# One queued vector task, not two, behind the turn that follows a mixing step of the attention stage

## The chip, the cores and the metric

The kernel runs on one core of one Trainium2 chip. The metric is the device time of one execution in microseconds (us): the median of several executions. TensorE (PE, with PEld for its weight loads) multiplies matrices, VectorE (DVE) and ScalarE (ACT) work on tiles element by element, GpSimd (POOL) and SyncE (SP) mostly issue transfers. Each engine works off its own queue in order, and the engines wait for each other through semaphores.

## The reference

One encoder layer on 512 tokens of width 2048, all in float32. One input projection gives queries, keys, values and gates of two groups of 16 heads. Group A attends along dilated windows, group B in a two-dimensional neighbourhood; each result is multiplied by a SiLU gate, both go through one output projection, and a residual layer norm follows.

```python
h = jnp.einsum('bsd,de->bse', x, w_in[layer])
qa, ka, va, ga, qb, kb, vb, gb = jnp.split(h, splits, axis=-1)
ya = _dilated_attention(heads(qa, N_HEADS_A), heads(ka, N_HEADS_A), heads(va, N_HEADS_A), t5_bias)
yb = _neighbourhood_attention(heads(qb, N_HEADS_B), heads(kb, N_HEADS_B), heads(vb, N_HEADS_B), na_rpb[layer])
ya = merge(ya) * jax.nn.silu(ga.astype(jnp.float32))
yb = merge(yb) * jax.nn.silu(gb.astype(jnp.float32))
y = jnp.concatenate([ya, yb], axis=-1).astype(x.dtype)
out = jnp.einsum('bse,ed->bsd', y, w_out[layer])
x = _layer_norm(DEEPNORM_ALPHA * x + out, ln_gain[layer], ln_bias[layer])
```

## The kernel before

Float32 operands are kept as two parts, a high one and a low one (`split`: the high part is a rounded copy made by ACT, the low part the remainder made by DVE), and a product is three matmuls: high times high, high times low, low times high.

The program has three stages. The first computes the projections (lines 279 to 407 of the matmuls). The second, from 595.5 us on, is the attention stage, which the change touches. The third finishes the output projection and the layer norm.

The attention stage is one loop over 136 steps, `n`. A step handles a quarter of a head: 128 queries. Four steps are a head, eight are a pair of heads, `i = n // 8`; pairs of group A (all 512 keys a query block) and of group B (192 or 256 keys) alternate. Step n holds, in the order of the code:

- the scores of quarter n: two matmuls (lines 677 and 678) into one PSUM bank `sc`, then on DVE one instruction that adds the bias, writes `s` and gives the row minimum `mn` (line 634), and on ACT the exponential (line 638);
- in a mixing step (n % 4 == 2) the weighted values of the head that ended: eight matmuls into a bank `pv` (line 719), a copy of half of it by ACT to `tmp` (line 864), and the sum of both halves by DVE to `y` (line 865);
- the turn of quarter n - 2: the probabilities are transposed on PE into a bank `pt` (line 697), ACT copies them to `th` (line 702), and DVE makes the remainder `tl` (line 703);
- some matmuls of a filler stream (lines 572 and 778): first six gate projections, then the first half of the output projection. They take weights that are loaded ahead and split by ACT (`wh`, line 549) and DVE (`wl`, line 553).

`sc` and `pv` take turns in the same two PSUM banks. So scores need the bank that the bank user before the last one has left free: either line 634 has read that step's scores, or line 865 has read the values.

Small DVE tasks that belong to no step stand in a list `held`, ordered by rank. Rank 1 is the low part of a weight (line 553) and the second half of a gate's SiLU (line 578). Rank 2 is the division of `y` by the softmax denominators (line 751) and the low part of the gated `y` (line 759, which writes the tile `yk`). Rank 4 is the product of `y` with its gate (line 742). `behind_min(k)` takes up to k tasks from the front and issues them at that place of the DVE queue. There are two such places in a group of four steps: a mixing step takes two, between its softmax and its line 865; the step behind it (n % 4 == 3) takes one or two, right behind the low part of its turn. How many the second place takes is the line that changes (872). One more rule sets the latest place of a weight's low part: `prepare`, called before the first matmul of each weight, issues what is due and not done yet.

The engines of this stage are scheduled by hand (`manual_schedule`): instructions stand in each engine's queue as the code issues them.

Of the kernel before, what the change touches and what calls it, by code (L numbers as in the profile page):

```python
# [71 lines left out]
def hybrid_layer(tc, xT, xn, w_in, w_early, w_mid, w_gate, w_out, t5x, brow, rpb, cmask, eye, gain, lbias, out):  # L72
    nc = tc.nc
    from contextlib import ExitStack
    with ExitStack() as ctx:
# [452 lines left out]
        held = []  # L528

        def later(k, fn, dve=False):  # L530


            tasks.setdefault(step[0] + k, []).append((fn, dve))

        def prepare():

            while lows_due:
                low = lows_due.pop(0)
                low()
                held[:] = [h for h in held if h[1] is not low]  # L540
            while stream and len(raws) < 4:
                raws.append(raw_ring.next("wraw"))
                nc.sync.dma_start(raws[-1], stream.pop(0))
            if not raws:
                return
            raw = raws.pop(0)
            h, l = halves.next("wh", F32R), halves.next("wl", F32R)
            ready.append((h, l))
            later(1, lambda: nc.scalar.activation(h, raw, AF.Copy))

            def low():
                if not done:
                    nc.vector.tensor_tensor(l, raw, f(h), ALU.subtract)
                    done.append(True)

            done = []
            lows_due.append(low)
            later(1 if step[0] % 4 else 2, low, 1)
# [31 lines left out]
        def load_kq(i):  # L590

            g, j = ORDER[i]
            t0 = 4 * (i % 2)
            kt = slot(f"t{t0}", F32R, "k").rearrange("p (a n) -> p a n", a=2)
            qt = slot(f"t{t0 + 1}", F32R, "q").rearrange("p (a n) -> p a n", a=2)
            ql = lows[i % 2]

            nc.sync.dma_start(f(kt.rearrange("p a n -> p (a n)")), k_d[g][j].rearrange("c s a q -> (c s) (a q)"))
            for a in range(2):
                nc.sync.dma_start(f(qt[:, a]), _view(q_d[g], (256 * j + 64 * a) * S, [[S, 64], [0, 2], [1, S]]))  # L600
            nc.sync.dma_start(f(ql[0:128:2]), q_d[g][j][1].rearrange("(a c) q -> c a q", a=2))
            loaded[i] = qt, ql, kt

        def load_v(i):


            g, j = ORDER[i]
            vv = slot(f"t{4 * (i % 2) + 2}", F32R, "vv").rearrange("p (b e) -> p b e", b=4)
            if g == 0:
                nc.sync.dma_start(f(vv.rearrange("p b e -> p (b e)")), v_d[g][j].rearrange("p b e -> p (b e)"))  # L610
            else:
                at = j * 128 * 1024
                for p0, c0, n, col, blk in ((0, 0, 4, 8, 0), (64, 0, 3, 0, 1), (64, 3, 1, 0, 0)):
                    nc.sync.dma_start(f(vv[p0:p0 + 64, c0:c0 + n].rearrange("p b e -> p (b e)")),
                                      _view(v_d[g], at + 1024 * col + 256 * blk,
                                            [[16 * 1024, 8], [1024, 8], [1, 256 * n]]))
            vs[i] = vv.rearrange("p b (h e) -> p b h e", h=2)

        def load_sg(i):
            sgs[i] = sg_ring.next("sg")  # L620
            nc.sync.dma_start(sgs[i], sg_d[i])
# [35 lines left out]
        def load_bias(h):  # L657
            g, _, _, hg = head(h)
            bias = two[h % 2]
            n = BW if g else 560  # L660
            nc.sync.dma_start(bias[:, :n], bias_d[g][hg])
            biases[h] = bias

        def scores(n):

            h, b = divmod(n, 4)
            g, i, a, _ = head(h)
            qt, ql, kt = loaded[i]
            cols = slice(128 * b, 128 * b + 128)
            sc = bank(pss, "sc")  # L670
            o, ko = sc, kt[:, a]
            if g:
                rows = "p (r w) -> p r w"
                c0, w = COLS[b]
                o = sc[:, :8 * w].rearrange(rows, r=8)
                ko = ko.rearrange(rows, r=8)[:, :, c0:c0 + w]
            nc.tensor.matmul(o, qt[:, a, cols], ko, start=True, stop=False)  # L677
            nc.tensor.matmul(o, ql[:, a, cols], ko, start=False, stop=True)  # L678
            if g == 0:
                p, exponent = softmax(sc, biases[h][:, 48 - 16 * b:560 - 16 * b], 512, 0, i, 4 * a + b)  # L680
                probs[n] = p, 4
                return exponent
            at = BIAS[(0, 1, 1, 2)[b]][0]
            outer = {0: (64, outers[h % 2][0]), 3: (0, outers[h % 2][1])}
            p, exponent = softmax(sc, biases[h][:, at:at + 8 * w].rearrange(rows, r=8), 8 * w, 1, i, 4 * a + b,
                                  *outer.get(b, ()))
            probs[n] = p, 2
            return exponent
# [36 lines left out]
        def share(i):  # L725

            turn8 = bank(pst, "pt")[0:8, 0:128]
            nc.tensor.transpose(turn8, dens[i], ident)
            rc = rc_ring.next("rc")

            def send():
                nc.scalar.activation(row, turn8, AF.Copy)
                nc.gpsimd.dma_start(rc_d[i], row)
                for a in range(2):
                    nc.gpsimd.dma_start(rc[64 * a:64 * a + 64], _view(rc_d, 1024 * i + 512 * a, [[0, 64], [1, 512]]))
                rcs[i] = rc

            later(0, send)
# [74 lines left out]
        def fill(n):  # L813
            for _ in range(n):
                next(filler, None)
# [4 lines left out]
        def behind_min(n):  # L820

            for _ in range(min(n, len(held))):
                held.pop(0)[1]()

        def close():

            for fn, dve in tasks.pop(step[0], ()):
                if dve and 0 <= step[0] < 134:
                    hold(dve, fn)
                else:  # L830
                    fn()
            step[0] += 1
# [5 lines left out]
        with tc.manual_schedule(engines=engines):  # L838
            prepare()
            for _ in range(3):  # L840
                close()
            while step[0] < 0:
                fill(7)
                close()
            for n in range(136):
                b, i = n % 4, n // 8
                mixing = n % 4 == 2 and 6 <= n <= 130
                amount = ((3, 5, 3, 5) if n < 76 else (5, 6, 4, 6))[b]
                if b == 0 and n < 124:
                    load_bias(n // 4 + 1)  # L850
                if n % 8 == 0 and n < 120:
                    load_kq(i + 1)
                if n % 8 == 4 and n < 128:
                    if n < 120:
                        load_v(i + 1)
                    load_sg(i)
                exponent = scores(n) if n < 128 else None
                if mixing:
                    if exponent:
                        exponent()  # L860
                    behind_min(2)
                    fill(2)
                    mine, theirs, y, t = values(n // 4 - 1)
                    nc.scalar.activation(t, theirs, AF.Copy)
                    nc.vector.tensor_tensor(y, mine, t, ALU.add)
                    fill(amount - 2)
                else:
                    fill(2)
                if 2 <= n < 130:
                    turn(n - 2)  # L870
                if b == 3 or n >= 134:
                    behind_min(99 if n >= 134 else 2 if len(held) > 3 or held and held[0][0] == 1 else 1)
                if not mixing:
                    if exponent:
                        exponent()
                    fill(amount - 2)
                if n >= 8 and n % 8 == 0:
                    later(0, lambda i=i: nc.vector.reciprocal(dens[i - 1], dens[i - 1]))
                if n >= 8 and n % 8 == 1:
                    share(i - 1)  # L880
                if n >= 8 and n % 8 == 4:
                    later(0, lambda i=i: gate(i - 1), 4)
                if n % 8 == 1 and 2 <= i < 2 * PAIRS:
                    gated(i - 2)
                if n % 8 == 7 and i >= 2 * PAIRS - 1:
                    gated(i - 1)
                close()
            for n in (0, 400):
                fill(n)
                while tasks or held:  # L890
                    behind_min(99)
                    close()
# [238 lines left out]
```

## Time and profile before

| | |
|---|---|
| median of 3 executions | 976.0 us (975.39 to 976.22) |
| the profiled execution's own time | 975.37 us |
| its span, first to last instruction | 973.6 us |
| attention loop, scores of step 0 to scores of step 127 | 595.51 to 862.90 us |
| mean granted TensorE clock | 0.998 |
| ACT, POOL busy, share of the span | 501.3 us (51%), 181.2 us (19%) |

A line of the profile's timeline is: start, duration, engine, source line, operation, the tile written and those read, and in brackets the idle time of the engine just before with what ended it. The duration of a matmul is modelled and overlaps with the next one, so that the distance of two starts tells more than the durations. The windows view gives for a stretch of time its length and what each engine was busy in it, with the number of instructions.

### The profile page before, as it was taken

The numbers are of one execution on the slowest core, as the hardware profiler recorded it, in microseconds if no ns is written. First come the engines' busy times: TensorE is split into PE (matmuls) and PEld (weight loads), VectorE is DVE, ScalarE is ACT, GpSimd is POOL, SyncE is SP. The second block draws the span as 40 slices with busy tenths as digits, with TensorE's granted clock in tenths as the row PEclk, the third lists the DMA queues.
The fourth block names the chain that finished last, engine by engine and source line by source line (L and its number), as shares of the span: only waits on it lengthen the run. The fifth ranks groups of instructions, "written<-read, shape, count | busy, mean of one in ns | idle before, by whom it ended". The sixth has DMA issues, their size and how long they took to land.

```text
span 973.6 us, 14211 instructions
## 1 busy us (share of the span) xinstructions
PE 964.5 (99%) x4861; PEld 805.3 (83%) x4861; DVE 767.2 (79%) x1169; ACT 501.3 (51%) x870; POOL 181.2 (19%) x321
## 2 busy tenths in 40 slices
PE   9999999999999999999999999999999999999997
PEld 7878888888888889998888888878888788888886
DVE  7897778779689678788679885788887777777877
ACT  7454444444444344454444544777776776763300
POOL 1006646735646000000000000111111010010020
PEclk9999999999999999999999999999999999999999
DMA  9716797698496086272196178767787668678213
GB/s 341 272 67 136 240 314 209 181 302 231 104 362 197 29 258 162 72 272 87 52 301 179 52 228 269 263 214 256 221 276 217 208 205 241 192 228 296 73 58 116
DMA packets 121255, 194.18 MB, mean 199 GB/s; under 512 B 49551, under 2 KB 70415, under 8 KB 121184
## 3 DMA queue, kind: packets, MB, share of 16 engines
q1 hardware_dynamic: 108672, 170.21, 54.8%
q0 software_dynamic: 11936, 22.42, 8.3%
q8 instruction: 38, 0.62, 0.3%
q10 hardware_dynamic: 576, 0.66, 0.2%
q14 instruction: 33, 0.27, 0.1%
HBM read 148.69 MB, written 44.50 MB: 198 GB/s over the span
## 4 chain that ended last, share of the span: by engine, by line
PE 94%; ACT 2%; DVE 2%; issue 1%; DMA 1%; SPq 0%; DVEq 0%; ACTq 0%
PE acc L405 16%; PE acc L407 16%; PE acc L406 16%; PE acc L778 14%; PE acc L572 6%; PE pv L719 4%; PE pt L697 4%; PE acc L397 2%; PE acc L396 2%; PE acc L395 2%; PE sc L678 2%; PE sc L677 2%; PE pt L260 1%; PE acc L279 1%; PE sc L778 1%; PE acc L280 1%
## 5 line engine op out<-in xcount | busy, mean ns | idle before, releaser
L377 ACT ACTIVATE wh<-braw 128x1024 fp32r<-128x1024 f32 (+1 forms) x196 | 202.1, 1031 | 278.9 <-PE acc L406 205.5
L382 DVE TENSOR_TENSOR wl<-braw,wh 128x1024 fp32r<-128x1024 f32 (+1 forms) x196 | 232.8, 1190 | 59.7 <-ACT wh L377 59.4
L405 PE MATMUL acc<-wh,xk 128*128 128x512 f32 x384 | 151.5, 394 | 0.0
L407 PE MATMUL acc<-wl,xk 128*128 128x512 f32 x384 | 149.9, 390 | 0.0
L406 PE MATMUL acc<-wh,xk 128*128 128x512 f32 x384 | 149.7, 390 | 0.0
L373 DVE TENSOR_TENSOR braw<-braw 128x1024 f32<-128x1024 f32 (+1 forms) x112 | 132.3, 1182 | 0.0
L778 PE MATMUL acc<-wh,yk 128*128 128x512 f32 x320 | 113.5, 407 | 0.0
L405 PE MATMUL acc<-wh,op 128*128 128x512 f32 x288 | 113.3, 393 | 0.0
L407 PE MATMUL acc<-wl,op 128*128 128x512 f32 x288 | 112.4, 390 | 0.0
L406 PE MATMUL acc<-wh,op 128*128 128x512 f32 x288 | 112.2, 390 | 0.0
L703 DVE TENSOR_TENSOR tl<-pt,th 128x256 fp32r<-128x256 f32 (+1 forms) x128 | 71.1, 556 | 29.8 <-ACT th L702 27.9
L407 PEld LDWEIGHTS acc<-wl,xk 128*128 128x128 f32 x384 | 72.1, 188 | 15.3
L405 PEld LDWEIGHTS acc<-wh,xk 128*128 128x128 f32 x384 | 72.2, 188 | 15.2 <-ACT bias L151 0.9
L406 PEld LDWEIGHTS acc<-wh,xk 128*128 128x128 f32 x384 | 72.2, 188 | 14.4
L638 ACT ACTIVATE p<-s,mn 128x512 f32<-128x512 f32 (+1 forms) x96 | 62.5, 651 | 32.9 <-DVE mn L634 32.2
L634 DVE CUSTOM_DVE_ANT_0 s<-sc,biases 128x512 f32<-128x512 f32 (+2 forms) x128 | 67.6, 528 | 11.3 <-PE sc L678 10.9
L702 ACT ACTIVATE th<-pt 128x256 fp32r<-128x256 f32 (+1 forms) x128 | 62.2, 486 | 22.6 <-PE pt L697 21.0
L778 PEld LDWEIGHTS acc<-wh,yk 128*128 128x128 f32 x320 | 58.1, 189 | 8.2 <-ACT wh L88 0.2
L161 POOL DMA_DIRECT2D bias<-rows_d x128 | 61.4, 487 | 15.8 <-DMA rows_d<-bias 5.4
L407 PEld LDWEIGHTS acc<-wl,op 128*128 128x128 f32 x288 | 54.1, 188 | 11.4
L406 PEld LDWEIGHTS acc<-wh,op 128*128 128x128 f32 x288 | 54.2, 188 | 10.9
L405 PEld LDWEIGHTS acc<-wh,op 128*128 128x128 f32 x288 | 54.1, 188 | 10.9
(188 smaller groups left out, 1777.7 us busy)
## 6 DMA issues: line engine op xcount, KB each, us to landing
braw<-in_w_in SPq DMA_DIRECT2D x96, 512.0 KB
wraw<-in_w_out SPq DMA_DIRECT2D x32, 512.0 KB
k_d<-kst SPq DMA_DIRECT2D x64, 128.0 KB
q_d<-kst SPq DMA_DIRECT2D x64, 128.0 KB
v_d<-vst SPq DMA_DIRECT2D x32, 256.0 KB
q<-q_d SPq DMA_DIRECT2D x32, 256.0 KB
k<-k_d SPq DMA_DIRECT2D x16, 512.0 KB
braw<-in_w_mid SPq DMA_DIRECT2D x16, 384.0 KB
```

Source lines behind the costliest of these rows:

```text
L161: nc.gpsimd.dma_start(bt[16 * r:16 * r + 16], _view(rows_d, h * 16 * ROW + 463 - 64 * r, [[ROW - 1, 16], [1, 560]]))
L373: nc.vector.tensor_tensor(raws[q][u], raws[q][u], raws[other][u], ALU.add)
L377: nc.scalar.activation(h, raws[q][u], AF.Copy)
L382: nc.vector.tensor_tensor(l, raws[q][u], f(h), ALU.subtract)
L405: nc.tensor.matmul(accs[t], ah[:, q], h[:, c], start=first and k == 0, stop=False, skip_group_check=skip)
L406: nc.tensor.matmul(accs[t], al[:, q], h[:, c], start=False, stop=False, skip_group_check=skip)
L407: nc.tensor.matmul(accs[t], ah[:, q], l[:, c], start=False, stop=k == 7, skip_group_check=skip)
L634: nc.vector.tensor_tensor_reduce(*flat, bias, 1.0, 3e38, ALU.add, ALU.min, mn)
L638: nc.scalar.activation(p[:, to:to + n].rearrange("p (b r c) -> p b r c", r=8, c=c), s[:, :n].rearrange(order, r=8, c=c), AF.Exp, bias=mn, ...
L702: nc.scalar.activation(th, pt[:, :nch], AF.Copy)
L703: nc.vector.tensor_tensor(tl, pt[:, :nch], f(th), ALU.subtract)
L778: nc.tensor.matmul(acc[:, part], yk[k][:, s, c], w[:, wk], start=first and kk == 0 and n == 0, stop=last and kk == 1 and n == 2)
```

## The change

One condition of the attention loop: how many tasks the step behind a mixing step takes.

```diff
@@ -869,7 +869,7 @@
                 if 2 <= n < 130:
                     turn(n - 2)
                 if b == 3 or n >= 134:
-                    behind_min(99 if n >= 134 else 2 if len(held) > 3 or held and held[0][0] == 1 else 1)
+                    behind_min(99 if n >= 134 else 2 if len(held) > 3 and held[0][0] > 1 else 1)
                 if not mixing:
                     if exponent:
                         exponent()
```

Before, the place takes two tasks if the first of the list has rank 1 (or if more than three wait). After, it takes two only if more than three wait and the first isn't of rank 1. The list never holds more than three tasks here, so it always takes one.

Where the list begins with a task of rank 1 and holds a second one, that second task now goes to the next place. This is so at seven steps: 3, 19, 43, 67, 83, 107 and 115. At step 3 the list is the SiLU half and a weight's low part; at the other six it is a weight's low part and the low part of a `y`. All other instructions of DVE, and all of PE, ACT, POOL and SP, stand as before.

DVE from step 19 to the mixing step 22, before; the first row is the low part of a weight behind the turn of step 19:

```order
L553 TENSOR_TENSOR wl_5763<-wraw_5337,wh_5762 128x1024
L759 SCALAR_TENSOR_TENSOR yk_5768<-y_5487,yk_5768 128x512
L634 ISA s_5839,mn_5841<-sc_5836,biases_5241 128x512
L634 ISA mn_5841 128x1
L703 TENSOR_TENSOR tl_5797<-pt_5845,th_5796 128x4x128
L634 ISA s_5857,mn_5859<-sc_5854,biases_5241 128x512
L634 ISA mn_5859 128x1
L703 TENSOR_TENSOR tl_5797<-pt_5863,th_5796 128x4x128
L634 ISA s_5877,mn_5879<-sc_5874,biases_5241 128x512
L634 ISA mn_5879 128x1
L742 TENSOR_TENSOR y_5689<-y_5689,sg_5631 128x512
L865 TENSOR_TENSOR y_5894<-pv_5885,tmp_5250 64x512
```

The same place of DVE after the change:

```order
L553 TENSOR_TENSOR wl_5763<-wraw_5337,wh_5762 128x1024
L634 ISA s_5838,mn_5840<-sc_5835,biases_5241 128x512
L634 ISA mn_5840 128x1
L703 TENSOR_TENSOR tl_5797<-pt_5844,th_5796 128x4x128
L634 ISA s_5856,mn_5858<-sc_5853,biases_5241 128x512
L634 ISA mn_5858 128x1
L703 TENSOR_TENSOR tl_5797<-pt_5862,th_5796 128x4x128
L634 ISA s_5876,mn_5878<-sc_5873,biases_5241 128x512
L634 ISA mn_5878 128x1
L759 SCALAR_TENSOR_TENSOR yk_5768<-y_5487,yk_5768 128x512
L742 TENSOR_TENSOR y_5689<-y_5689,sg_5631 128x512
L865 TENSOR_TENSOR y_5894<-pv_5885,tmp_5250 64x512
```

The low part of `y` (L759) has moved over the softmax rows of steps 20, 21 and 22 and the turns of steps 20 and 21, into the mixing step, where the gate product (L742) stands already. The same happens from step 43 to 46, 67 to 70, 83 to 86, 107 to 110 and 115 to 118.

DVE from step 3 to the mixing step 6, before; the first row is the second half of a gate's SiLU:

```order
L578 SCALAR_TENSOR_TENSOR sgo_5335<-sgo_5335,acc_5274 128x512
L553 TENSOR_TENSOR wl_5340<-wraw_5268,wh_5339 128x1024
L634 ISA s_5429,mn_5431<-sc_5426,biases_5241 128x512
L634 ISA mn_5431 128x1
L703 TENSOR_TENSOR tl_5386<-pt_5435,th_5385 128x4x128
L634 ISA s_5447,mn_5449<-sc_5444,biases_5241 128x512
L634 ISA mn_5449 128x1
L703 TENSOR_TENSOR tl_5386<-pt_5453,th_5385 128x4x128
L634 ISA s_5471,mn_5473<-sc_5468,biases_5241 128x512
L634 ISA mn_5473 128x1
L865 TENSOR_TENSOR y_5487<-pv_5478,tmp_5250 64x512
```

And after:

```order
L578 SCALAR_TENSOR_TENSOR sgo_5335<-sgo_5335,acc_5274 128x512
L634 ISA s_5428,mn_5430<-sc_5425,biases_5241 128x512
L634 ISA mn_5430 128x1
L703 TENSOR_TENSOR tl_5386<-pt_5434,th_5385 128x4x128
L634 ISA s_5446,mn_5448<-sc_5443,biases_5241 128x512
L634 ISA mn_5448 128x1
L703 TENSOR_TENSOR tl_5386<-pt_5452,th_5385 128x4x128
L553 TENSOR_TENSOR wl_5340<-wraw_5268,wh_5339 128x1024
L634 ISA s_5471,mn_5473<-sc_5468,biases_5241 128x512
L634 ISA mn_5473 128x1
L865 TENSOR_TENSOR y_5487<-pv_5478,tmp_5250 64x512
```

The low part of weight 3 (L553) has moved over two steps to the end of step 5, where `prepare` issues it ahead of the weight's first matmul.

## The prediction

> **What bounds the kernel now.** I read the page first, then the stage's windows, then the chain of waits and the timeline at one place.
>
> ```profile
> PE 964.5 (99%) x4861; PEld 805.3 (83%) x4861; DVE 767.2 (79%) x1169; ACT 501.3 (51%) x870; POOL 181.2 (19%) x321
> PE 94%; ACT 2%; DVE 2%; issue 1%; DMA 1%; SPq 0%; DVEq 0%; ACTq 0%
> ```
>
> PE is busy for 99% of the span and makes up 94% of the chain that ended last. So time is won only where PE has to wait, and work that DVE does beside a busy PE costs nothing. The change moves DVE work at seven places and leaves every other queue in its order. The question is whether PE waits behind it there.
>
> To see that, I cut the stage at the first score matmul of a step and take two steps at a time: the one ahead of a mixing step and the mixing step. The PE work of such a pair repeats every 16 steps, so that pairs with and without a doubled DVE task can be laid side by side. The first column after the window is its length, the second PE's busy time.
>
> ```profile
> core 0: us, PE busy (x) PEld busy (x) DVE busy (x) ACT busy (x) POOL busy (x), PEclk, DMA share, GB/s
> 603.47:609.03 5.56, 5.56 (x30) 4.38 (x28) 4.08 (x9) 3.73 (x9) 0.59 (x1) 1.00 0.95 229
> 667.52:673.02 5.50, 5.50 (x30) 4.38 (x28) 4.42 (x10) 4.67 (x11) 1.18 (x3) 1.00 0.72 213
> 699.85:705.25 5.40, 5.40 (x29) 4.45 (x28) 4.51 (x11) 4.32 (x10) 0.00 (x0) 1.00 0.79 198
> 635.09:641.42 6.33, 5.98 (x29) 4.29 (x28) 5.43 (x11) 3.76 (x9) 1.06 (x2) 1.00 0.74 212
> 731.31:737.64 6.33, 5.98 (x29) 4.30 (x28) 5.43 (x11) 3.75 (x9) 1.06 (x2) 1.00 0.75 219
> 652.65:656.28 3.63, 3.63 (x25) 3.20 (x24) 2.94 (x10) 2.98 (x10) 0.00 (x0) 1.00 0.91 231
> 684.25:688.64 4.39, 3.92 (x25) 3.10 (x24) 4.18 (x12) 2.19 (x10) 1.06 (x2) 1.00 1.00 311
> 803.52:809.36 5.84, 5.84 (x32) 4.82 (x30) 4.13 (x10) 4.72 (x10) 0.00 (x0) 1.00 0.91 213
> 766.54:773.31 6.77, 6.41 (x32) 4.68 (x30) 5.67 (x12) 4.08 (x11) 0.00 (x0) 1.00 0.89 207
> 839.56:845.75 6.19, 6.11 (x32) 4.76 (x30) 5.15 (x12) 4.05 (x10) 0.00 (x0) 1.00 0.95 205
> 786.36:790.46 4.10, 4.10 (x28) 3.57 (x26) 3.02 (x8) 3.04 (x9) 0.00 (x0) 1.00 0.73 242
> 822.41:826.51 4.10, 4.10 (x28) 3.57 (x26) 2.65 (x10) 2.43 (x8) 1.05 (x2) 1.00 1.02 362
> ```
>
> In order these are the steps 5+6, 37+38, 53+54, then 21+22 and 69+70; 29+30, then 45+46; 101+102, then 85+86 and 117+118; 93+94, then 109+110. The pairs named behind "then" follow the steps 19, 67, 43, 83, 115 and 107, where a weight's low part and a `y`'s low part are issued together. They are longer than a pair of the same work by 6.33 - 5.50 = 0.83 us twice, 4.39 - 3.63 = 0.76, 6.77 - 5.84 = 0.93, 6.19 - 5.84 = 0.35 and 4.10 - 4.10 = 0: together **3.70 us**, and nearly all that this stage loses to DVE in such pairs.
>
> The chain of waits inside the first of them shows the mechanism (start, length, engine and line):
>
> ```profile
> 634.99 0.74 DVE wl L553
> 635.73 0.39 issue
> 636.12 0.69 DVE yk L759
> 636.80 0.60 DVE s L634
> ...
> 637.51 0.82 ACT p L638 x2
> 638.33 0.49 ACT th L702
> ...
> 638.86 2.14 PE pv L719 x8
> ```
>
> The low part of the weight and then that of `y` stand ahead of the softmax of step 20. Its end lets ACT take the exponential and then `th`, for which the values matmul of PE waits. The `y` task has nothing that PE needs here; it only stands in the way.
>
> **The change part by part.** It adds and removes no instruction. It moves six times line 759 and once line 553.
>
> What does one place win by losing line 759? Not its own 0.69 us:
>
> ```profile
> 636.12 0.69 DVE L759 SCALAR_TENSOR_TENSOR yk<-y,yk 128x512 fp32r<-128x512 f32 x1
> 636.72 0.68 DVE L634 CUSTOM_DVE_ANT_0 s<-sc,biases 128x512 f32<-128x512 f32 x1
> ```
>
> The next instruction starts 636.72 - 636.12 = 0.60 us after it, so a task shifts what is behind it by 0.60 us. I take 0.60 per place, where the pair lost more than that: four places, 4 x 0.60 = 2.40 us. Where less was lost, all of it comes back: 0.35 at 117+118, 0 at 109+110. The sum is **2.75 us**. What the four pairs lost beyond 0.60 (0.23 twice, 0.16, 0.33) I leave standing, since the weight's low part is still there and takes 636.12 - 634.99 = 1.13 us of the queue.
>
> The Trainium skill, page VectorE: DVE Perf Modes, section The DRAIN you can't avoid, says that the next op does not start until the pipe of the one before is empty; it also sends the reader on to a case in which a next op starts earlier. By its first sentence a place would win a whole duration, and the two rows above disagree, as the next one starts 0.09 us ahead of the end. It is a rival below.
>
> Now the other end of the move. Line 759 lands in the mixing step, ahead of line 742 and of line 865, whose end frees the values' bank for the scores two steps on. Does it fit there? Line 865 waits for ACT's copy `tmp` anyway; the first, the shortest and the last of the six waits:
>
> ```profile
> 641.70 0.68 DVE L865 TENSOR_TENSOR y<-pv,tmp 64x512 f32<-64x512 f32 x1 [0.96 <-ACT tmp L864]
> 689.45 0.68 DVE L865 TENSOR_TENSOR y<-pv,tmp 64x512 f32<-64x512 f32 x1 [0.75 <-ACT tmp L864]
> 845.76 0.68 DVE L865 TENSOR_TENSOR y<-pv,tmp 64x512 f32<-64x512 f32 x1 [1.05 <-ACT tmp L864]
> ```
>
> 0.60 us go into 0.75 us or more. As DVE reaches this point earlier by as much as PE does, the wait keeps its size where both move by 0.60. So I cost the landing at nothing; uncovered it would be 0.60 at each of six places. The same pair of tasks stands in a mixing step of the kernel before already (step 30), and a longer pair too (step 38):
>
> ```profile
> 655.05 0.69 DVE L759 SCALAR_TENSOR_TENSOR yk<-y,yk 128x512 fp32r<-128x512 f32 x1
> 655.65 0.68 DVE L742 TENSOR_TENSOR y<-y,sg 128x512 f32<-128x512 f32 x1
> 656.74 0.68 DVE L865 TENSOR_TENSOR y<-pv,tmp 64x512 f32<-64x512 f32 x1 [0.40 <-ACT tmp L864]
> ...
> 671.70 0.68 DVE L578 SCALAR_TENSOR_TENSOR sgo<-sgo,acc 128x512 f32<-128x512 f32 x1
> 672.30 1.22 DVE L553 TENSOR_TENSOR wl<-wraw,wh 128x1024 fp32r<-128x1024 f32 x1
> 673.43 0.68 DVE L865 TENSOR_TENSOR y<-pv,tmp 64x512 f32<-64x512 f32 x1
> ```
>
> Step 30 still waits 0.40 us for `tmp`, and its pair is the 3.63 us of the table. Step 38 waits no more, and its pair, 5.50 us, is no longer than the others. Nobody needs the low part of `y` in between: its reader is the output projection, at the earliest at step 77 for the task that now comes at step 70.
>
> The other move is line 553 for weight 3, from step 3 to the end of step 5:
>
> ```profile
> 604.74 0.40 SPq L543 DMA_DIRECT2D wraw<-in_w_gate  x1
> 611.33 0.32 SPq L661 DMA_DIRECT2D biases<-biasb_d  x1
> 609.33 0.68 DVE L865 TENSOR_TENSOR y<-pv,tmp 64x512 f32<-64x512 f32 x1 [1.56 <-ACT tmp L864]
> ```
>
> It relieves pair 5+6, which is 5.56 us against 5.40 in the shortest like it: at most 0.16 us to win. It lands ahead of the softmax of step 6, in a step whose line 865 waits 1.56 us: its 1.13 us are covered, and lost in full if they weren't. I take 0, the nearest row being the 1.56. PE needs this low part only 16 matmuls into the weight, some steps later. The load of the next raw weight into its buffer waits on SP for it and would be issued about 3 us later than 604.74; the next issue of SP stands at 611.33, so nothing is held up.
>
> After the loop everything is shifted as a whole, as no transfer there is started by a clock of its own.
>
> The sum against the profiled execution: 975.37 - 2.75 = 972.62 us. That execution lies 0.63 below the median, so against the runs it is 976.0 - 2.75 = 973.25: **973.2 us**.
>
> **The rivals.**
>
> *Only the idle that PE's rows show.* The five long pairs leave PE idle, length less busy time, 0.35, 0.35, 0.47, 0.36 and 0.08 us, together 1.61. If matmuls truly took the time that they are shown with, no more could come back: 976.0 - 1.61 = 974.4, within 0.2%. Against it stands that 3.70 us of length are missing where 1.61 are idle, with the same matmuls. The Trainium skill, page Perfetto Trace Analysis, section Identifying the Most-Contended Engine, says that matmul busy time is a poor measure because matmuls are pipelined; the pairs above agree. A weaker form with nearly the same time: the weight's low part alone still holds the softmax up, and some 1.2 to 1.6 us come back.
>
> *A whole duration per task.* 4 x 0.69 + 0.35 = 3.11, so 972.9 us. For it: a last instruction of a row counts with its end. Against it: the 0.60 us between two starts. The sentence of the Trainium skill on the pipe, above, would give this result.
>
> *All gaps close.* 3.70 us, 972.3: if waits at two places of a pair were caused by one task and fall together, as the lost 0.93 at 85+86 exceeds the task.
>
> *The wait comes back one step later.* In the mixing step two tasks together reach past `tmp`, line 865 frees the bank late, and the scores behind it wait.
>
> ```profile
> PEld sc L677 <- DVE y L865: 0.4, 2, 0.2
> ```
>
> This wait exists, at two places, with 0.2 us at most. It decides from the point at which the room ahead of line 865 falls below 0.60 us; the least is 0.75. Priced as the dearest queue of this stage, 0.93 at each of the six places, it costs 5.58 and with the 2.75 won leaves 976.0 + 2.83 = 978.8 us, slower.
>
> That the change doesn't do what it says is excluded by the order of DVE's queue, where the seven moves stand.
>
> **How the numbers follow.** The forecast has 0.60, the whole duration 0.10, all gaps 0.08, the idle alone with its weaker form 0.17, the wait that comes back 0.05. A measurement of this kernel can tell about 0.2%, 1.95 us, from no change. The first three, 0.78 together, lie beyond it, though the forecast by only 0.8 us: for the scatter I move 0.02 of them to no change. So faster 0.76, same 0.19, slower 0.05. The forecast's own bounds are 2.1 us (0.60 as above with one of the four places failing) and 3.7; with the 0.4 us by which the runs scatter, 971.9 to 974.3. To hold 8 in 10 the range reaches to the idle's 974.4 with the same scatter: **971.9 to 974.8**.
>
> **What would show it.** Windows of the same six pairs in the new profile should be 5.5 to 5.75 (twice), 3.65 to 3.8, 5.85 to 6.2, 5.85 and 4.1 us. Line 759 should stand between lines 634 and 742 of steps 22, 46, 70, 86, 110 and 118, and line 865 behind it should still wait for `tmp`, by 0.1 us or more. Steps 5+6 should keep their 5.4 to 5.6. I'm wrong if the pairs keep their length while line 759 is gone from them (then the weight's low part alone is the cause), or if they shrink and the pairs behind them, from the step after the mixing step, grow.

## The result, and the profile after

| | before | after |
|---|---|---|
| median, us | 975.88 (974.97 to 977.13, 15 runs) | 973.87 (972.80 to 974.77, 15 runs) |
| ratio | | 0.9978 (95%: 0.9970 to 0.9986) |
| profiled execution, us | 975.37 | 973.54 |
| span, us | 973.6 | 971.8 |

The change makes the kernel faster by 0.22%, about 2.1 us. Forecast was 973.2, 2.75 below the kernel before.

The busy times have moved little (PE from 964.5 to 963.0 us, DVE from 767.2 to 768.5 us), and the change can't be read from them. The windows show it, cut as before at the first score matmul of a step. These are the changed kernel's pairs 5+6, 9+10, 21+22, 69+70, 45+46, 85+86, 117+118, 109+110, and last the loop from the scores of step 0 to those of step 127:

```profile
603.90:609.29 5.39, 5.39 (x30) 4.45 (x28) 4.17 (x9) 3.31 (x8) 0.59 (x1) 1.00 0.78 234
612.80:618.13 5.33, 5.03 (x28) 3.92 (x27) 3.49 (x11) 3.11 (x11) 0.54 (x1) 1.00 0.92 296
635.84:641.54 5.70, 5.68 (x29) 4.37 (x28) 5.43 (x11) 3.73 (x9) 1.06 (x2) 1.00 0.75 205
730.85:736.56 5.71, 5.69 (x30) 4.38 (x28) 5.43 (x11) 3.73 (x9) 1.07 (x2) 1.00 0.85 206
684.34:688.14 3.80, 3.80 (x25) 3.10 (x24) 3.59 (x12) 2.21 (x10) 1.06 (x2) 1.00 0.98 310
765.48:771.65 6.17, 6.13 (x31) 4.75 (x30) 5.67 (x12) 4.08 (x11) 0.00 (x0) 1.00 0.78 222
837.90:843.73 5.83, 5.83 (x32) 4.83 (x30) 5.15 (x12) 4.06 (x10) 0.17 (x1) 1.00 0.88 194
820.76:824.85 4.09, 4.09 (x27) 3.56 (x26) 2.83 (x8) 2.37 (x8) 0.24 (x1) 1.00 0.87 307
595.94:860.88 264.94, 264.56 (x1468) 219.26 (x1466) 207.63 (x502) 195.22 (x474) 27.20 (x51) 1.00 0.72 229
```

And of the kernel before the two that the prediction didn't show, pair 9+10 and the loop:

```profile
612.54:617.38 4.84, 4.84 (x28) 3.91 (x27) 3.03 (x10) 3.10 (x10) 0.54 (x1) 1.00 0.95 338
595.51:862.90 267.39, 265.79 (x1468) 219.01 (x1466) 207.43 (x502) 195.26 (x474) 27.22 (x51) 1.00 0.72 227
```

The five long pairs are shorter by 0.63, 0.62, 0.59, 0.60 and 0.36 us, 2.80 in all, and 109+110 stays. Pair 5+6 is 0.17 shorter. But pair **9+10**, at which nothing was moved, is 0.49 longer. The loop is 267.39 - 264.94 = 2.45 us shorter. In this execution the first stage took 0.43 us longer, with the same instructions in the same order (the loop starts at 595.94, not 595.51), and what lies behind the loop 0.19 longer, so that of 2.45 us only 1.83 are seen in its time.

The waits of PE's weight loads inside the loop (in all, how often, the longest), first before and then after, show where the time came from:

```profile
PEld pv L719 <- ACT th L702: 2.9, 6, 0.6
PEld sc L677 <- DVE mn L634: 2.7, 4, 0.9
```

```profile
PEld pv L719 <- ACT th L702: 1.6, 4, 0.5
PEld sc L677 <- DVE mn L634: 0.3, 1, 0.3
```

Two kinds of wait stand in the long pairs, not one. The values matmul waits for `th`, as the prediction's chain has it (not in 45+46); and the scores of the mixing step wait until the delayed softmax has read their bank (not in 117+118). Most of the second kind is gone.

The landing, on DVE in the mixing step 22 of the changed kernel (timeline; in brackets the idle time and what ended it):

```profile
640.20 0.69 DVE L759 SCALAR_TENSOR_TENSOR yk<-y,yk 128x512 fp32r<-128x512 f32 x1
640.80 0.68 DVE L742 TENSOR_TENSOR y<-y,sg 128x512 f32<-128x512 f32 x1
641.85 0.68 DVE L865 TENSOR_TENSOR y<-pv,tmp 64x512 f32<-64x512 f32 x1 [0.36 <-ACT tmp L864]
```

Line 865 still waits for `tmp`: the 0.96 us of before less 0.60.

### The profile page after: what moved, and what is told of

It reads as the page before. It is cut to its first block, busy times and chain, and to the rows that moved or that the text cites. A ratio compares the mean times of both kernels' runs of the same rounds, so it can differ in the third digit from the quotient of the medians.

```text
span 971.8 us, 14211 instructions
## 1 busy us (share of the span) xinstructions
PE 963.0 (99%) x4861; PEld 804.6 (83%) x4861; DVE 768.5 (79%) x1169; ACT 501.3 (52%) x870; POOL 181.6 (19%) x321
## 4 chain that ended last, share of the span: by engine, by line
PE 97%; DMA 1%; DVE 1%; ACT 0%; issue 0%; SPq 0%; DVEq 0%; ACTq 0%
PE acc L405 16%; PE acc L407 16%; PE acc L406 16%; PE acc L778 16%; PE acc L572 6%; PE pv L719 4%; PE pt L697 4%; PE sc L678 2%; PE sc L677 2%; PE acc L397 2%; PE acc L396 2%; PE acc L395 2%; PE pt L260 1%; PE acc L279 1%; PE sc L778 1%; PE acc L280 1%
## 5 line engine op out<-in xcount | busy, mean ns | idle before, releaser
L405 PE MATMUL acc<-wh,op 128*128 128x512 f32 x288 | 113.1, 393 | 0.0
```

Source lines behind the costliest of these rows:

```text
L405: nc.tensor.matmul(accs[t], ah[:, q], h[:, c], start=first and k == 0, stop=False, skip_group_check=skip)
```

## The experiments

Loop lengths below are those of one profiled execution each. They are the measure here, as two executions of the changed kernel differ by 0.04 us in the loop (264.94, and 264.90 in the eighth run) while times of whole executions scatter by 2 us. A whole time is set against the kernel before on the same chip.

**1. The six moves without that of weight 3.** In the changed kernel:

```diff
-                    behind_min(99 if n >= 134 else 2 if len(held) > 3 and held[0][0] > 1 else 1)
+                    behind_min(99 if n >= 134 else 2 if n == 3 else 1)
```

> The six moves of a y's low part alone; the low part of weight 3 goes back to step 3. Theory: the loop (scores of step 0 to scores of step 127, 267.38 us before, 264.93 after the change) holds a gain of 2.81 at the five pairs and a loss of about 0.3 from the weight's move (0.17 won in pair 5+6, 0.46 lost in pair 9+10). So pair 9+10 goes from 5.33 back to 4.84, pair 5+6 from 5.39 back to 5.55, the other pairs stay as after the change, and the loop is 264.6, 0.3 shorter than with the whole change. Rival: the 0.46 in pair 9+10 is chance or has another cause; then pair 9+10 stays at 5.33 and the loop at 264.9 or above.

Measured: 973.53 us (972.46 to 974.06, 7 runs) against 976.22, ratio 0.9971 (0.9960 to 0.9982). Its pairs 5+6 and 9+10, and its loop:

```profile
603.40:608.98 5.58, 5.58 (x30) 4.37 (x28) 4.08 (x9) 3.77 (x9) 0.59 (x1) 1.00 0.89 258
612.49:617.36 4.87, 4.87 (x28) 3.92 (x27) 3.03 (x10) 3.11 (x10) 0.54 (x1) 1.00 0.98 333
595.45:860.09 264.64, 264.56 (x1467) 219.16 (x1466) 207.57 (x502) 195.25 (x474) 27.21 (x51) 1.00 0.73 229
```

Both pairs are back, and the loop is 0.30 us shorter than with the whole change.

**2. The move of weight 3 alone.** In the kernel before:

```diff
-                    behind_min(99 if n >= 134 else 2 if len(held) > 3 or held and held[0][0] == 1 else 1)
+                    behind_min(99 if n >= 134 else 2 if n != 3 and held and held[0][0] == 1 else 1)
```

> The other half: the low part of weight 3 alone is moved, the six y tasks stand as before the change. Theory: pair 9+10 5.33, pair 5+6 5.39, the pairs 21+22, 45+46, 69+70, 85+86, 117+118 long as before (6.33, 4.39, 6.33, 6.77, 6.18), loop 267.38 + 0.3 = 267.7. Rival (no cause in the weight's move): pair 9+10 4.84 and loop 267.4 or below.

Measured, pairs 5+6 and 9+10 and the loop:

```profile
606.78:612.16 5.38, 5.38 (x29) 4.45 (x28) 4.16 (x9) 3.30 (x8) 0.59 (x1) 1.00 0.81 227
615.68:621.00 5.32, 5.03 (x28) 3.92 (x27) 3.48 (x11) 3.11 (x11) 0.54 (x1) 1.00 0.91 315
598.82:866.57 267.75, 265.84 (x1468) 218.97 (x1466) 207.43 (x502) 195.19 (x474) 27.21 (x51) 1.00 0.71 226
```

0.18 us won and 0.48 lost, without any of the six moves; the loop is 0.36 longer than before. So the loss belongs to weight 3, and the two halves of the change nearly add up: -2.75 (run 1) and +0.36 make -2.39, against -2.45 for both. Its single time, 978.90 us, tells nothing of the change: the first stage ended 3.3 us late, at 598.82 (see the last section).

**3. The task doubled where it was.** The kernel before, the `y`'s low part issued twice at the six places:

```diff
+                    again = held[1][1] if n in (19, 43, 67, 83, 107, 115) else None
                     behind_min(99 if n >= 134 else 2 if len(held) > 3 or held and held[0][0] == 1 else 1)
+                    again and again()
```

> The kernel before with the y's low part issued twice at the six places (the second time writes the same values). Theory: a task delays what is behind it by the 0.60 us between two starts, and where the pair already waits all of it reaches PE: 21+22 6.93, 45+46 4.99, 69+70 6.93, 85+86 7.37, 117+118 6.78, and 109+110, which had some room, 4.1 to 4.7; loop 267.38 + 3.0 to 3.6 = 270.4 to 271.0. Rival, a whole duration each: 0.69 in place of 0.60, 7.02 for the first. Rival, the pair of two tasks matters and not the length of the queue: no pair grows by more than 0.1, loop 267.4.

Measured, pairs 21+22, 85+86, 109+110 and the loop:

```profile
636.06:643.11 7.05, 5.97 (x29) 4.29 (x28) 6.14 (x12) 3.74 (x9) 1.06 (x2) 1.00 0.76 225
769.73:777.23 7.50, 6.40 (x31) 4.67 (x30) 6.37 (x13) 4.08 (x11) 0.00 (x0) 1.00 0.82 209
826.34:830.43 4.09, 4.09 (x27) 3.56 (x26) 3.24 (x11) 2.32 (x8) 0.70 (x2) 1.00 1.02 346
596.45:867.55 271.10, 266.00 (x1468) 218.80 (x1466) 211.43 (x508) 195.26 (x474) 27.31 (x51) 1.00 0.71 223
```

The loop grew by 3.71 us: five pairs by 0.70 to 0.74 each, the sixth not at all. That is more than the 0.60 of the theory, and the timeline of DVE shows what the queue grew by:

```profile
637.11 1.41 DVE L759 SCALAR_TENSOR_TENSOR yk<-y,yk 128x512 fp32r<-128x512 f32 x2
638.43 0.68 DVE L634 CUSTOM_DVE_ANT_0 s<-sc,biases 128x512 f32<-128x512 f32 x1
```

The two take 638.43 - 637.11 = 1.32 us of the queue, so the second adds 1.32 - 0.60 = 0.72. It writes what the first one writes, and both together are busy for 1.41, twice 0.69 and a gap of 0.03: it started when the first had ended, not 0.09 us before. What the queue grew by, PE lost at each of the five places, so the length of the queue matters, against the second rival. But the figure that the theory gave for the first pair, 6.93, missed the measured 7.05, and the first rival's 7.02 is nearer. As the doubled task follows one that writes the same values, this run can't tell 0.60 from 0.69 us for the task of the change; the four places of the change do (0.59 to 0.63).

**4. The task doubled where it lands.** The changed kernel, with the `y`'s low part twice in the six mixing steps:

```diff
+                    if n in (22, 46, 70, 86, 110, 118): held[0][1]()
                     behind_min(2)
```

> The changed kernel with the y's low part issued twice in the six mixing steps. Line 865 there waits for its copy by 0.36, 0.15, 0.36, 0.36, 0.40 and 0.69 us after the change; with 0.60 more ahead of it, it comes up to 0.45 late at five of them. Theory: it costs PE next to nothing, since the bank that line 865 frees is needed only two scores on; pairs as after the change, the steps behind them no more than 0.1 longer, loop 264.9 to 265.3. Rival, the wait comes back one step later: every 0.1 that line 865 is late is lost, 0.24 + 0.45 + 0.24 + 0.24 + 0.20 = 1.4, loop 266.3 or more.

The loop of this run and its steps 47+48 (the two behind a mixing step of group B):

```profile
688.26:691.76 3.50, 3.33 (x20) 2.46 (x18) 3.46 (x10) 2.40 (x8) 0.00 (x0) 1.00 0.66 207
595.88:861.42 265.54, 264.95 (x1467) 219.18 (x1466) 210.83 (x508) 195.30 (x474) 27.32 (x51) 1.00 0.72 228
```

The same steps of the changed kernel, and then, from the timeline of this run, the copy, line 865 and the weight load of the scores that waited:

```profile
688.14:691.20 3.06, 3.06 (x20) 2.50 (x18) 2.90 (x9) 2.45 (x9) 0.00 (x0) 1.00 0.75 230
```

```profile
688.42 0.60 ACT L864 ACTIVATE tmp<-pv 64x512 f32<-64x512 f32 x1
689.55 0.68 DVE L865 TENSOR_TENSOR y<-pv,tmp 64x512 f32<-64x512 f32 x1
690.27 0.19 PEld L677 LDWEIGHTS sc<-k,q 128*128 128x128 f32 x1 [0.61 <-DVE y L865]
```

0.60 us in all, between the theory's 0 to 0.4 and the rival's 1.4. Of it 0.44 lies in these two steps: line 865 started 0.53 us after `tmp` was there (689.55 against 688.42 + 0.60; the second task takes 0.72 us of the queue here too, not the expected 0.60), and the scores of step 48 waited for its bank. In the mixing steps 22, 70, 86 and 110 line 865 started 0.28 to 0.32 us after `tmp`, and the two steps behind them took no longer than in the changed kernel. Of the rest, 0.12 lies in pair 25+26, where the load for the values matmul waits 0.3 us for `th`. So the rival of the prediction, the wait that comes back behind the mixing step, is real, but it begins only beyond what one task needs.

**5. Why pair 9+10 waits.** The chain of waits of the changed kernel ahead of it, from the moved task on (start, length, engine and line):

```profile
606.73 1.20 DVE wl L553
607.92 0.60 DVE s L634
...
609.47 0.60 ACT tmp L864
...
610.09 0.60 ACT th L702
610.69 0.95 ACT wh L549
611.63 0.49 ACT th L702
...
612.76 0.67 DVE wl L553
...
614.86 0.12 DVE den L878
...
615.11 0.27 PE pt L728
```

Reading down: the low part of weight 3 delays the softmax of step 6; this delays ACT's exponential and so `tmp`, `th` and the high part of weight 4; this delays the turn of step 7 and the low part of weight 4 on DVE; and behind all that comes the reciprocal of the first pair's denominators (line 878), for which PE's transpose (line 728) waits. Counted from the start of the loop, the softmax of step 6 starts 0.33 us later than in the kernel before (607.84 - 595.94 against 607.08 - 595.51), and the reciprocal 0.29 us later (614.77 against 614.05). Line 865 of step 6 waits for `tmp` as long as before the change, 1.56 us, and starts 0.34 us later, counted in the same way (609.33 before):

```profile
610.10 0.68 DVE L865 TENSOR_TENSOR y<-pv,tmp 64x512 f32<-64x512 f32 x1 [1.56 <-ACT tmp L864]
```

The later load of a raw weight isn't part of the chain: the high part of weight 4 (line 549) follows directly on line 702. In this run the transpose of that pair came one step later:

```diff
-                if n >= 8 and n % 8 == 1:
+                if n >= 8 and n % 8 == (2 if n < 16 else 1):
                     share(i - 1)
```

> The changed kernel, with the transpose of the first pair's softmax denominators (line 728) moved from step 9 to step 10. It asks how the weight's move loses 0.46 in pair 9+10. Theory: the late softmax of step 6 makes ACT's work behind it late, then the low part of weight 4 on DVE, then the reciprocal of the denominators, and line 728 waits for that reciprocal; moved back by one step it finds it ready. Pair 9+10 goes from 5.33 to 4.9 or below and no pair behind it grows; loop 264.5. Rival: DVE is late as a whole there and PE waits for it at the next place (the scores of step 10 or the values): pair 9+10 stays at 5.2 to 5.4.

Measured, pairs 9+10 and 11+12, the loop, and from the timeline two waits of weight loads, in step 10 and in step 11:

```profile
613.44:618.49 5.05, 5.05 (x28) 3.97 (x27) 3.49 (x11) 3.06 (x10) 0.00 (x0) 1.00 0.90 312
618.49:621.53 3.04, 3.04 (x19) 2.31 (x17) 2.18 (x7) 2.30 (x8) 0.54 (x1) 1.00 0.62 212
596.58:861.46 264.88, 264.80 (x1467) 219.20 (x1466) 207.82 (x502) 195.48 (x474) 27.31 (x51) 1.00 0.72 229
```

```profile
616.06 0.77 PEld L719 LDWEIGHTS pv<-th,vv 128*128 128x128 f32 x4 [0.35 <-ACT th L702]
619.41 0.20 PEld L697 LDWEIGHTS pt<-ident,p 128*128 128x128 f32 x2 [0.42 <-ACT tmp L732]
```

The wait of step 9 was the transpose's: PE goes on to the scores of step 10 without it, and PE's idle time in the pair (5.33 - 5.03 without this edit) is gone. But the pair is 5.05, not 4.9, the next one is longer by 0.20 (2.84 after the change), and the loop is as long as without this edit. In step 10 the load for the values matmul now waits 0.35 us for `th`, which it does not do in the changed kernel, and in step 11 the bank of the turns waits for its copy by ACT (line 732). So the place of the wait is shown, but the rival is half right: without the transpose in the way PE waits at the next place, the values, and the copy that belongs to the moved transpose holds up a turn. Moving the transpose is no remedy.

**6 and 7. The other task of the two moved.** In the changed kernel the `y`'s low part stays behind the turn at three steps, and the weight's goes to the mixing step; run 7 also leaves weight 3 at step 3:

```diff
-                    behind_min(99 if n >= 134 else 2 if len(held) > 3 and held[0][0] > 1 else 1)
+                    held.pop(1)[1]() if n in (19, 43, 67) else behind_min(99 if n >= 134 else 1)
```

with `2 if n == 3 else 1` in run 7 in place of the last `1`.

> At the steps 19, 43 and 67 the other task of the two is moved: the y's low part stays behind the turn and the weight's low part goes to the mixing step. All else as after the change. Theory: the weight's low part takes 1.13 us of the queue where the y's takes 0.60, so what is left of the long pairs goes too: 21+22 and 69+70 from 5.70 to 5.5, 45+46 from 3.80 to 3.64. At the landing line 865 comes later by 0.53 than after the change, with 0.36, 0.15 and 0.36 of room: 0.2 lost behind step 46, nothing behind 22 and 70. Loop 264.93 - 0.56 + 0.2 = 264.6. Rival: what is left in those pairs isn't the weight's doing; they stay at 5.70 and 3.80 and the loop at 264.9 to 265.2.

> The version that the runs point to: the weight's low part moved instead of the y's at 19, 43 and 67, the y's moved at 83, 107 and 115 as in the change, weight 3 left at step 3. Theory: pairs as in the run before this one, pair 9+10 4.85, 5+6 5.56; loop 264.3, 3.1 us below the kernel before, so about 0.9968 of its time, and some 0.6 below the changed kernel. Rival (what is left isn't the weight's doing): loop 264.6 to 264.9.

Run 6, pairs 21+22, 45+46, 69+70 and the loop:

```profile
636.45:641.84 5.39, 5.39 (x30) 4.45 (x28) 5.17 (x11) 3.80 (x9) 1.06 (x2) 1.00 0.66 214
684.66:688.32 3.66, 3.66 (x25) 3.22 (x24) 3.45 (x11) 2.52 (x11) 1.06 (x2) 1.00 1.03 342
731.03:736.42 5.39, 5.39 (x29) 4.45 (x28) 5.17 (x11) 3.80 (x9) 1.07 (x2) 1.00 0.79 200
596.57:860.74 264.17, 263.80 (x1468) 219.51 (x1466) 207.59 (x502) 195.43 (x474) 27.31 (x51) 1.00 0.73 230
```

The pairs have the length of the shortest without a doubled task (5.40, 3.63 before), 0.77 us of the loop in all. So what the change left standing there was the weight's low part. The landing cost nothing, not even the 0.2 expected behind step 46: line 865 came 0.29 us after `tmp` there (689.03 against 688.15 + 0.59 on ACT), and steps 47+48 took 3.07 us as against 3.06. With run 4: 0.29 late is free, 0.53 costs 0.44.

Run 7 had a loop of 263.92, 0.4 below what was expected, as run 6 had already been 0.4 below its own expectation; its time was 973.26 us (972.01 to 975.15, 7 runs) against 975.80, ratio 0.9970 (0.9958 to 0.9981).

**8 and 9. The changed kernel and run 7's version on one chip.** Nothing but run 7's line differs. The kernel before had medians of 975.80 to 976.22 us in the four measurements.

> The changed kernel once more, beside the next run on the same chip, as the difference of the two (1.0 us by their loops, 264.94 against 263.92) is smaller than the distance of medians from different chips. Expected: 0.9978 of the kernel before, as in the first measurement; loop 264.9.

> The version with the weight's low part moved at 19, 43 and 67 and weight 3 left in place, once more. Theory: loop 263.9, and a median 1.0 us below the changed kernel of the same call. Rival: what the loop wins comes back elsewhere; then both have the same median within 0.3 us.

| | median, us | ratio (95%) |
|---|---|---|
| before | 975.91 (975.51 to 976.85, 14 runs) | |
| the change | 973.60 (973.08 to 975.72, 10 runs) | 0.9977 (0.9968 to 0.9987) |
| run 7's version | 972.45 (972.32 to 973.16, 5 runs) | 0.9965 (0.9952 to 0.9977) |

The loop of the last one:

```profile
596.21:860.12 263.91, 263.84 (x1468) 219.46 (x1466) 207.51 (x502) 195.50 (x474) 27.30 (x51) 1.00 0.72 229
```

263.91 against 264.90 for the change, and medians 1.15 apart. The version beats both kernels by the loops and the medians; the two ratios' intervals overlap.

## Why the prediction was right, and where it was off

*What bounds the kernel.* Right. The six moves alone took 2.75 us off the loop (run 1), and the five long pairs hold all of it; of the two kinds of wait in them the prediction's chain names only the one for `th`.

*0.60 us per place.* Right, and the main term: 0.63, 0.62, 0.59 and 0.60 at the four pairs that lost more than that, 0.36 for 0.35 at 117+118, nothing at 109+110; 2.80 for 2.75. What was said to remain there, 0.23 twice, 0.16 and 0.33, remained: 0.20, 0.21, 0.17 and 0.33 over the pairs 5.50, 5.50, 3.63 and 5.84. Run 3 doesn't bear on the size, as its doubled task took 0.72. That the weight's low part is its cause was argued there; run 6 shows it for three of the four.

*The landing at nothing.* Right. The `y` tasks land behind the softmax of the mixing step, so that `tmp` doesn't stand behind them. The waits of line 865 shrank by what the task takes, 0.96 to 0.36 us in step 22, and no pair behind a mixing step with a moved `y` task grew by more than 0.02. Runs 4 and 6 give the point from which it would have cost: between 0.29 and 0.53 us of delay past `tmp`, in the steps of group B. The chance given to the wait that comes back was small for the right reason, since 0.75 of room was more than 0.60.

*Weight 3 at nothing.* This is the mis-sized term, and the sum's only one. The prediction set the cost of the move to 0 because line 865 of step 6 waits 1.56 us. The measured cost is +0.3 to +0.36: 0.17 won in pair 5+6 (the 0.16 named as the most that could be won), 0.46 to 0.49 lost in pair 9+10. Three edits show it, the whole change, the move alone and the rest without it. The wait of 1.56 us was the wrong cover. It belongs to an instruction that itself waits for ACT, and ACT's copy waits for the exponential of the delayed softmax; with that, line 865 waited as long as before, 1.56 us, and yet came 0.34 us later. The delay ran on through ACT's queue (`tmp`, `th`, the high part of weight 4) to DVE, and met PE three steps later, where a reciprocal stands behind a weight's low part. What pair 5+6 won was not kept: PE came to pair 9+10 earlier by 0.17 and found the reciprocal later by 0.29, which together are 0.46 of the 0.49. The bound of 1.13 us on the other side held.

*The rivals.* Only the idle that PE's rows show: 1.61 us against 2.80 at those pairs, so it falls, and with it the reading of a matmul's busy time as work; its time, 974.4, was the nearest to the median of 973.87 by accident. The Trainium skill, page Perfetto Trace Analysis, section Identifying the Most-Contended Engine, says that matmul busy time is not a good measure of how close a kernel is to roofline, as matmuls are pipelined. The pairs agree in that the time shown isn't work alone: the same matmuls are shown with 5.98 us in the pair of 6.33 and with 5.50 in that of 5.50. The weaker form, 1.2 to 1.6 us with the weight's low part still holding the softmax up, falls by the same 2.80. A whole duration per task: the change's own places have 0.59 to 0.63, not 0.69. All gaps close: not by this change, but by that of run 6 at three of four. The wait one step later: not with one task, only with the two of run 4.

*The sum.* 2.80 + 0.17 - 0.49 = 2.48 us, and the loop lost 2.45. Of the median it is 2.0 us, by the ratio 2.1 (1.4 to 2.9): the loop's 2.45 lies inside.

## What to carry to other kernels

Where the busiest engine waits behind a queue, the gain of moving a task away is its distance from start to start in that queue, and stops at what the engine lost there; lay stretches of the same work with and without the task side by side to see both. A wait of an instruction is room for a task only if what it waits for doesn't itself stand behind that task: follow the chain from the moved task to the end of every queue that it passes, not to the next wait. And of two tasks that stand in the way, move the longer one if the landing has room.

## What the runs showed of the hardware

A DVE instruction of 512 columns is shown with 0.69 us, but the next one started 0.60 us after it where it had no part in the first one's result, and 0.72 us after it where it wrote the same tile (run 3). The Trainium skill, page VectorE: DVE Perf Modes, section The DRAIN you can't avoid, says that the next op doesn't start until the pipe is empty, and that a next op which is not held starts earlier. The start after 0.72 us agrees with the first statement and that after 0.60 us with the second. That writing the same tile is what held the one back is likely, but no run took it apart.

Loops repeat to 0.04 us in the two versions that were profiled twice; whole executions do not. Most of the difference lies ahead of the loop, in the first stage: over the eleven profiles, with the same program there, the loop starts at 595.45 to 598.82 us, while what is left of an execution's time without that start and the loop is 112.3 to 113.1 us. In the kernel before (start of the loop 595.51), PE's first matmul on a weight waited 0.2 us, and the granted clock, the column ahead of the last two, was 1.00 over the first 45 us. That wait and these 45 us in run 2 (start of the loop 598.82):

```profile
PE acc L279 <- ACT wh L88: 2.5, 1, 2.5
```

```profile
0.00:45.00 45.00, 41.11 (x170) 32.18 (x171) 36.31 (x78) 26.00 (x55) 2.61 (x9) 0.96 0.87 308
```

And in run 8 (start of the loop 596.95):

```profile
PE acc L279 <- ACT wh L88: 2.3, 1, 2.3
```

```profile
0.00:45.00 45.00, 41.36 (x178) 32.97 (x179) 37.65 (x82) 27.63 (x58) 2.62 (x9) 1.00 0.87 317
```

The two waited nearly alike, and only in run 2 was the clock lower. So the wait alone doesn't bring the lower clock. The two profiles with 0.96 over these 45 us, those of the runs 2 and 7, are the two whose loop starts latest, 598.82 and 598.47; 4% of 45 us is about 1.8 us by estimate, and run 2 starts its loop 1.87 us behind run 8. What decides whether the clock falls stays open.
